# A hybrid attention layer on one core: maxima from a score pass of their own, exponentials with keys on the partitions

## The chip, the cores and the metric

The kernel runs on one core of one Trainium2 chip. The metric is the device time of one execution in microseconds (us), the median of several runs. TensorE (PE) multiplies matrices, VectorE (DVE), ScalarE (ACT) and GpSimd (POOL) do elementwise work, SyncE (SP) issues the DMAs.

## What is computed

One decoder layer over 2048 tokens of width 1024, in float32. A normalised input goes through one combined projection; three groups of heads read it: a causal pooling mixer, eight heads of forgetting attention, and four heads of cross-attention to 256 memory tokens. Each group is gated, the results are joined and go through an output projection, and the input is added.

```python
q = rms_norm(to_heads(q_b, FOX_HEADS), fox_q_g[l])        # 8 heads of 64
logits = einsum('bhqd,bhkd->bhqk', qi, k) * scale
logits = logits + Fi[..., None] - F[:, :, None, :]        # F = cumsum(log forget gate)
logits = where(causal, logits, -1e30)
p = softmax(logits, axis=-1)                              # one maximum and one sum per query
out = einsum('bhqk,bhkd->bhqd', p, v)
```

The memory heads do the same without F and mask. The scales of the norms are large, so the scores are too, and every softmax needs the maximum of its row.

## The kernel before, in words

Every float32 operand is split in two float16 halves (hi and lo), and a product is made of three matmuls (hi·hi, hi·lo, lo·hi), so that TensorE works in float16.

The work is cut into 16 units: four passes p over the columns of the projection (two attention heads, one memory head and one pooling group in each), and in each four blocks j of 512 queries. For a unit, `proj` makes q, k, v and gates of 512 tokens (line 714 has its matmuls, tiles pa and pb); `transpose_in` brings q and k into Q and K with the head's dimension on the partitions, by DMA transposes; then `attention` goes over three heads, h = 2 (memory), 0 and 1.

For one head `pieces` cuts the scores into pieces of up to 1024 columns, each in a buffer q of PSUM of which there are two ("qk": 2). `scores` fills it with queries on the partitions: for up to 512 keys one matmul of the high halves (line 1139, contraction 67: 64 dimensions and three rows with the forget sums F), one with the other halves (line 1144), and on the diagonal one that adds the mask (line 1142). `soften` finds the minimum of the negated scores per query on VectorE (line 1160; line 1156 for memory heads), makes a bias nm of it (lines 1164 and 1168), and takes the exponential on ScalarE with that bias (line 1175) into p, float32. `halves` writes p as ph: a cast by ScalarE or VectorE (lines 1195 and 1198) and a subtraction by VectorE or GpSimd (line 1202). Since the product with V needs keys on the partitions, ph goes through a DMA transpose into pt on SP's queue (line 1208). `weigh` multiplies pt and V, three matmuls of 64 or 65 columns per block of 128 queries by 128 keys (lines 1238 to 1240), into pv. Heads with more than 1024 keys do this in two parts with two biases, merged by `part` and `finish` (lines 1257 and 1272).

The order of all instructions is written by a planner, `Order`, before the program is built. It keeps a clock for each engine, with costs from a table, and two streams: `lead` (projections, then the output projection) and `follow` (attention), which may lag 1.1 units behind. A stream that has nothing ready lets the other go. Each engine then runs its instructions in that order, and an instruction that waits holds all behind it on its engine.

```python
COST = {"A": (0.08, 0.00086), "V": (0.07, 0.00105), "G": (0.1, 0.002), "C": (0.07, 0.00053), "S": (0.0, 1.0 / 360e3)}
...
            t = o.use("V", w // 2)
```

The table (line 39) gives microseconds, fixed and per column, of ScalarE (A), VectorE (V), GpSimd (G) and a cast on VectorE (C, by which an engine is chosen; line 1196, quoted second, is what that cast is then charged).

Of the kernel before, what the change touches and what calls it, by code (L numbers as in the profile page):

```python
# [10 lines left out]
F32 = mybir.dt.float32  # L11
# [25 lines left out]
ONE = 2.0 ** 14  # L37

# [162 lines left out]
class Layer:  # L201
    DEEP = 7
    BUFS = {
        "x": 3, "st": 4, "w": 2, "b": 2, "pj": 2, "qk": 2, "pv": 2, "p32": 3, "ph": 5, "pt": 6, "qkr": 2, "qsq": 2,
        "gate": 7, "z": 3, "kk": 1, "Q": 2, "cs": 2, "pw": 1, "hy": 3, "band": 1, "rx": 4, "cs2": 2, "early": 3, "late": 2, "scaled": 1,
# [19 lines left out]
    def setup(self):  # L225
# [33 lines left out]
        self.qq = kv.tile([P, 3, 4, P], F16, name="qq")  # L259
        self.fd = self.dr.tile([3 * NF, S], F16, name="fd")  # L260
# [497 lines left out]

    def mem_heads(self):
# [36 lines left out]
        def rest():  # L796
# [28 lines left out]
            nc.gpsimd.memset(self.Km[HD:HD + 3, 0], 0.0)  # L825
# [178 lines left out]
    def transpose_in(self, n, gates, normed):  # L1004
        nc, o = self.nc, self.o
        p, j = divmod(n, NJ)
        if p == 0:
            yield from self.wait(("forget", j))
        yield from o.until(lambda: 0 in normed and 1 in normed)
        if n > 0:  # L1010
            yield from self.wait("mem")
        else:
            yield from self.wait(("x", 1, 0))
            yield from self.wait(("x", 1, 1))
            yield from self.wait(("x", "mem", 0))
# [4 lines left out]
        Q, K = self.Q[n % 2], self.K[n % (NJ + 1)]  # L1020
        fs = self.fd[6 * p:6 * p + 6, j * TB:(j + 1) * TB].rearrange("(h c) s -> c h s", c=3)
# [6 lines left out]
        if n < 2:  # L1028
            nc.gpsimd.memset(Q[HD:HD + 3, 0], -1.0)
            nc.gpsimd.memset(Q[HD:HD + 1, 0], -1024.0)  # L1030
            o.use("G", 0, 1.5)
# [86 lines left out]
    def scores(self, n, h, piece, qk):  # L1118
# [7 lines left out]
        for i, k0, w, off in piece:  # L1126
            q1, q2 = Q1[:, h, i * P:(i + 1) * P], Q2[:, h, i * P:(i + 1) * P]
            for b in range(0, w, TB):
# [10 lines left out]
                nc.tensor.matmul(out, q1, kb, start=bank not in used, stop=False, **kw)  # L1139
                used.add(bank)  # L1140
                if diag:
                    nc.tensor.matmul(out[:, bw - P:], self.identb, self.mask, start=False, stop=False, **kw)
                    cost += 0.056
                nc.tensor.matmul(out, q2, ka, start=False, stop=True, **kw)  # L1144
                cost += 2 * bw / 2400.0 + 0.006
# [43 lines left out]
    def halves(self, n, h, c, w, p32, pt, place, head):  # L1189
# [14 lines left out]
        o.give(pt)  # L1204
        tt = yield from o.claim(place[2])
# [7 lines left out]
    def weigh(self, job):  # L1213
# [5 lines left out]
        g = piece[0][1] // HK  # L1219
# [7 lines left out]
        end = c == head["count"] - 1 or head["flat"][c + 1][0][1] // HK != g  # L1227
        T, nb, tt = head["box"].pop(c)
        b = 0
        for i, k0, w, off in piece:  # L1230
            for s in range(k0 // P, (k0 + w) // P):
                if h < 2:
                    v = self.V[(p * NJ + s // 4) % (NJ + 2)][:, s % 4, h, :]
                else:
                    v = self.Vm[:, s, p, :]
                ph, pl = T[:, b, :], T[:, nb + b, :]
                hi = v[:, HD:2 * HD + 1]
                nc.tensor.matmul(pv[:, i, :], ph, hi, start=start and b == 0, stop=False, **kw)  # L1238
                nc.tensor.matmul(pv[:, i, 0:HD], ph, v[:, 0:HD], start=False, stop=False, **kw)  # L1239
                nc.tensor.matmul(pv[:, i, :], pl, hi, start=False, stop=end and b == nb - 1, **kw)  # L1240
                b += 1
                if b % 2 == 0 or b == nb:
                    yield 0.0885 * (2 - b % 2)
# [53 lines left out]
    def attention(self):  # L1297
# [12 lines left out]
        def ready():  # L1310
            return late and late[0][2] in late[0][-1]["box"]

        for n in range(n_units):
            p, j = divmod(n, NJ)
            while n not in self.att_in or (n == 0 and "mem" not in self.done):
# [4 lines left out]
            gates, qt = self.att_in.pop(n)  # L1320
            first = True
            for h in (2, 0, 1):
                pieces = self.pieces(j, h)
                subs, count = [], 0
                for piece in pieces:
                    subs.append([])
                    for sub in self.cut(piece):
                        subs[-1].append((count, sub))
                        count += 1
                head = {  # L1330
                    "mn": self.sm.tile([P, 2, 4], F32, tag="mn", bufs=3, name=f"mn{n}{h}"),
                    "nm": self.sm.tile([P, 2, 4], F32, tag="nm", bufs=3, name=f"nm{n}{h}"),
                    "pv": {}, "box": {}, "subs": subs, "count": count, "gates": gates, "last": h == 1,
                    "flat": [sub for group in subs for _, sub in group],
                }
                for c, piece in enumerate(pieces):
                    while not o.free_slot("qk") or len(late) > self.DEEP:
                        if ready():
                            yield from drain()
                        else:  # L1340
                            yield -0.05
                    tk = o.first("qk")
                    qk = self.ps_qk.tile([P, 1024], F32, tag="qk", name=f"q{n}{h}{c}")
                    cost = self.scores(n, h, piece, qk)
                    o.spawn(self.soften((n, h, c, piece, qk, tk, head)), cost + SEM)
                    late += [(n, h, k, sub, head) for k, sub in subs[c]]
                    yield cost
                    if first:
                        first = False
                        o.spawn(self.pool_mix(p, j, gates))  # L1350
                    if ready():
                        yield from drain()
            o.give(qt)
            self.scored = n + 1
            o.spawn(self.store_mixed(n, gates))
# [6 lines left out]
    def follow(self):  # L1362

        n, spent = 0, 0.0
        for c in self.attention():
            spent += max(c, 0.0)
            total = 0.203 * (8 + 2 * (16 * (n % NJ) + 10))
# [238 lines left out]
```

## Time and profile before

| | |
|---|---|
| median of 3 runs | 1105.33 us (1098.9 to 1107.97) |
| the profiled execution | 1104.63 us |
| its span, first to last instruction | 1102.8 us |
| mean granted TensorE clock | 0.977 of 2.4 GHz |
| busy: PE, DVE, ACT, POOL | 1000.0, 817.5, 562.1, 433.0 us |

The times of the trace are from the profiled execution, one run. A busy time counts an engine's bars; bars of matmuls overlap, since they are pipelined. A wait is idle time of an engine just before an instruction, put down to what released it.

### The profile page before, as it was taken

The page shows a single profiled execution, that of the slowest core. Times are in us where ns is not written, and L with a number is a line of the kernel's source. Part 1 is how long each engine was busy: PE and PEld are TensorE (multiplying, and loading weights), DVE is VectorE, ACT ScalarE, POOL GpSimd, SP SyncE. Part 2 cuts the span into 40 slices and gives each one's busy share as a digit, 9 for nine tenths or more (in the row PEclk, how much of TensorE's full clock was granted, in tenths as well). Part 3 has the DMA queues.
Part 4 walks back from the last instruction along what each step waited for, and adds up shares of the span by engine and source line. Part 5 has one row for each costly group of instructions (what it writes and reads, how often), then busy time and mean ns, then how long its engine had stood idle before and what let it go on. Part 6 is the DMA issues. An engine that isn't in the chain of part 4 may idle for free.

```text
span 1102.8 us, 23610 instructions
## 1 busy us (share of the span) xinstructions
PE 1000.0 (91%) x8693; PEld 600.3 (54%) x8693; DVE 817.5 (74%) x1895; ACT 562.1 (51%) x1453; POOL 433.0 (39%) x484
## 2 busy tenths in 40 slices
PE   6798897889889998888899899998898989999998
PEld 3455564556556555555566565565555644444443
DVE  5977577599889797978887868998788796762111
ACT  4775466466646474656564656664555553430000
POOL 5543534354343643434345445543444460221000
PEclk8899698999999999999999999999999999999999
DMA  9889889999899998998998889999999699998521
GB/s 284 208 221 198 205 217 205 240 220 172 163 213 191 231 241 157 176 202 157 202 194 232 176 188 198 206 205 194 219 251 218 148 170 244 225 225 224 191 95 49
DMA packets 485700, 219.33 MB, mean 199 GB/s; under 512 B 442128, under 2 KB 450256, under 8 KB 484560
## 3 DMA queue, kind: packets, MB, share of 16 engines
q1 hardware_dynamic: 485440, 217.81, 91.4%
q8 instruction: 68, 1.11, 0.4%
q14 instruction: 48, 0.39, 0.1%
q10 hardware_dynamic: 144, 0.01, 0.0%
HBM read 84.23 MB, written 25.26 MB: 99 GB/s over the span
## 4 chain that ended last, share of the span: by engine, by line
PE 23%; DMA 12%; DVE 11%; issue 2%; SPq 1%; ACT 1%; POOL 1%; DVEq 0%; ACTq 0%; POOLq 0%
PE po L714 12%; DMA pt<-ph 12%; PE pa L714 4%; PE pb L714 3%; DVE mn L1160 3%; DVE ph L1202 2%; DVE ph L1195 1%; PE pv L1238 1%; PE q L1139 1%; PE q L1144 1%; PE pv L1240 1%; PE pv L1239 1%; SPq L1208 1%; POOL ph L1202 1%; DVE qq L998 1%
## 5 line engine op out<-in xcount | busy, mean ns | idle before, releaser
L1175 ACT ACTIVATE p<-q,nm 128x512 f32<-128x512 f32 (+3 forms) x384 | 216.3, 601 | 168.0 <-DVE nm L1168 79.6
L714 PEld LDWEIGHTS <-x 128*128 128x128 f16 x2304 | 216.1, 98 | 130.1 <-issue 4.7
L714 PE MATMUL pa<-ah,x 128*128 128x512 f16 x768 | 250.1, 382 | 0.0
L1202 POOL TENSOR_TENSOR ph<-p,ph 128x512 f16<-128x512 f32 (+3 forms) x115 | 134.6, 1175 | 259.2 <-DVE ph L1195 148.3
L1238 PE MATMUL pv<-v,pt 128*128 128x65 f16 x1088 | 130.8, 194 | 56.5 <-DMA pt<-ph 56.1
L1160 DVE TENSOR_REDUCE mn<-q 128x1 f32<-128x128 f32 (+2 forms) x192 | 170.7, 902 | 6.8 <-PE q L1144 6.6
L1202 DVE TENSOR_TENSOR ph<-p,ph 128x512 f16<-128x512 f32 (+3 forms) x221 | 159.5, 732 | 18.1 <-ACT ph L1198 16.5
L1238 PEld LDWEIGHTS <-pt 128*128 128x128 f16 x1216 | 114.3, 99 | 105.0 <-DMA pt<-ph 89.9
L714 PE MATMUL po<-aho,om 128*128 128x512 f16 x512 | 157.9, 379 | 0.0
L714 PE MATMUL pa<-al,x 128*128 128x512 f16 x384 | 146.5, 381 | 0.0
L714 PE MATMUL pb<-bh,x 128*128 128x256 f16 x768 | 140.8, 273 | 1.6 <-DVE v L925 1.5
L1198 ACT CAST ph<-p 128x512 f16<-128x512 f32 (+3 forms) x168 | 97.2, 586 | 72.5 <-DMA pt<-ph 58.2
L1239 PE MATMUL pv<-v,pt 128*128 128x64 f16 x1088 | 130.3, 194 | 0.0
L1240 PE MATMUL pv<-v,pt 128*128 128x65 f16 x1088 | 129.9, 195 | 0.0
L1139 PE MATMUL q<-k,q 67*128 67x512 f16 (+2 forms) x320 | 111.1, 350 | 13.6 <-ACT p L1175 8.8
L1239 PEld LDWEIGHTS <-pt 128*128 128x128 f16 x1216 | 113.9, 98 | 16.8 <-issue 0.8
L714 PEld LDWEIGHTS <-om 128*128 128x128 f16 x768 | 73.3, 98 | 83.7
L1240 PEld LDWEIGHTS <-pt 128*128 128x128 f16 x1216 | 114.2, 98 | 0.0
L1144 PE MATMUL q<-k,q 128*128 128x512 f16 (+2 forms) x320 | 110.8, 349 | 0.0
L970 POOL TENSOR_TENSOR rr<-ss,mhalf 128x10 f32<-128x10 f32 x32 | 65.4, 2044 | 103.1 <-DVE ss L965 99.0
L714 PE MATMUL pb<-bl,x 128*128 128x256 f16 x384 | 105.0, 273 | 0.0
L1195 DVE CAST ph<-p 128x512 f16<-128x512 f32 (+3 forms) x168 | 77.2, 468 | 35.3 <-DMA pt<-ph 30.8
(244 smaller groups left out, 1750.0 us busy)
## 6 DMA issues: line engine op xcount, KB each, us to landing
x<-xd SPq DMA_DIRECT2D x48, 512.0 KB
xrx<-in_x SPq DMA_DIRECT2D x16, 512.0 KB
xd<-xx SPq DMA_DIRECT2D x16, 512.0 KB
md<-mt SPq DMA_DIRECT2D x32, 256.0 KB
om<-md SPq DMA_DIRECT2D x8, 1024.0 KB
xo<-in_x SPq DMA_DIRECT2D x16, 512.0 KB
out_dram<-xo SPq DMA_DIRECT2D x32, 256.0 KB
w0a<-in_w_a SPq DMA_DIRECT2D x12, 512.0 KB
```

The lines of the kernel that those rows point to most:

```text
L714: nc.tensor.matmul(out, rows, r[kt][:, :ncol], start=(kt == 0 and i == 0), stop=(kt == KT - 1 and i == 2))
L970: nc.gpsimd.tensor_tensor(rr, ss, self.mhalf[:, 0:10].rearrange("p (a b) -> p a b", b=5), op=ALU.pow)
L1139: nc.tensor.matmul(out, q1, kb, start=bank not in used, stop=False, **kw)
L1144: nc.tensor.matmul(out, q2, ka, start=False, stop=True, **kw)
L1160: nc.vector.tensor_reduce(mn[:, g, i:i + 1], qk[:, off:off + w], axis=AX.X, op=ALU.min)
L1175: nc.scalar.activation(p32[:, at:at + w], qk[:, off:off + w], AF.Exp, bias=nm[:, g, i:i + 1], scale=-1.0)
L1195: nc.vector.tensor_copy(hl[:, :w], p32[:, :w])
L1198: nc.scalar.copy(hl[:, :w], p32[:, :w])
L1202: (nc.vector if eng == "V" else nc.gpsimd).tensor_tensor(hl[:, w:2 * w], p32[:, :w], hl[:, :w], op=ALU.subtract)
L1238: nc.tensor.matmul(pv[:, i, :], ph, hi, start=start and b == 0, stop=False, **kw)
L1239: nc.tensor.matmul(pv[:, i, 0:HD], ph, v[:, 0:HD], start=False, stop=False, **kw)
L1240: nc.tensor.matmul(pv[:, i, :], pl, hi, start=False, stop=end and b == nb - 1, **kw)
```

## The change

Every head now has two score passes. The first (`scores` with `peak`) has the high halves and the mask alone, with queries on the partitions, and gives only the minima (`peak`). Two float16 rows are made of them (in a tile mz, 128 columns wide per block of queries), turned by four matmuls with an identity (tile mp), and copied into rows 96 and 97 of Q by ScalarE or VectorE; K has the matching constants there (`extra_rows`, memsets on GpSimd). The second pass (`turned_scores`) has keys on the partitions, all halves, and a contraction of 98 rows, so the maximum comes out subtracted; `spread` takes the exponentials with one constant bias, in full banks of 512 where it can. The halves ph are then read by `weigh` as weights; no pt is made of them and no DMA transpose is issued for them. A head has one part whatever its keys. The first pass of the next head goes ahead of the second pass of this one (AHEAD = 1). There are nine buffers ph in place of five.

```diff
-        "x": 3, "st": 4, "w": 2, "b": 2, "pj": 2, "qk": 2, "pv": 2, "p32": 3, "ph": 5, "pt": 6, "qkr": 2, "qsq": 2,
+        "x": 3, "st": 4, "w": 2, "b": 2, "pj": 2, "qk": 2, "pv": 2, "p32": 3, "ph": 9, "pt": 6, "qkr": 2, "qsq": 2,
...
+    def extra_rows(self, K):
+        nc, o = self.nc, self.o
+        nc.gpsimd.memset(K[HD:P, 0], 0.0)
+        nc.gpsimd.memset(K[MAX_ROW:MAX_ROW + 2, 0], 1.0)
+        nc.gpsimd.memset(K[MAX_ROW:MAX_ROW + 1, 0], 1024.0)
+        o.use("G", 0, 3.0)
...
+    def columns(self, j, h):
+        if h == 2:
+            return [[[(0, 0, TB)], [(1, 0, TB)]]]
+        k = 4 * j
+        full = [[[(b, 0, TB)], [(b + 1, 0, TB)]] for b in range(0, k, 2)]
+        return full + [[[(k, 0, TB)], [(k + 1, P, 3 * P), (k + 3, 3 * P, P)]], [[(k + 2, 2 * P, 2 * P)]]]
+
+    def turned_scores(self, n, h, piece, qk):
...
+                nc.tensor.matmul(out, k1, Q1[:, q0:q0 + w], start=i == 0, stop=False, **kw)
+                if h < 2 and kb >= 4 * j:
+                    nc.tensor.matmul(out[:, 0:P], self.mask, self.identb, start=False, stop=False, **kw)
+                nc.tensor.matmul(out, k2, Q2[:, q0:q0 + w], start=False, stop=True, **kw)
...
+    def peak(self, n, h, c, piece, qk, tk, head):
...
+                nc.vector.tensor_reduce(mn[:, g, i:i + 1], qk[:, off:off + w], axis=AX.X, op=ALU.min)
...
+        if g:
+            nc.vector.tensor_tensor(n0, n0, mn[:, 1, :], op=ALU.min)
+        nc.vector.tensor_scalar(mz[:, :, MAX_ROW], n0, -1.0 / 1024.0, None, op0=ALU.mult)
+        nc.vector.scalar_tensor_tensor(
+            mz[:, :, MAX_ROW + 1], mz[:, :, MAX_ROW], -1024.0, n0, op0=ALU.mult, op1=ALU.subtract
+        )
...
+        for t in range(4):
+            nc.tensor.matmul(mp[:, t * P:(t + 1) * P], mz[:, t], self.identh, start=True, stop=True)
...
+        (nc.scalar.copy if eng == "A" else nc.vector.tensor_copy)(self.Q[n % 2][rows, 0, h], mp[rows])
...
+    def spread(self, n, h, c, piece, qk, tk, head):
...
+            nc.scalar.activation(p32[:, :w], qk[:, b * TB:b * TB + w], AF.Exp, bias=self.lnp, scale=-1.0)
...
     def halves(self, n, h, c, w, p32, pt, place, head):
...
+        if head["turned"]:
+            head["box"][c] = (hl.rearrange("p (b c) -> p b c", c=P), w // P, ht)
+            return
...
+            for ahead in todo[:self.AHEAD + 1]:
+                if ahead["n"] not in self.att_in or (ahead["n"] == 0 and "mem" not in self.done):
+                    break
+                if ahead["todo"]:
+                    step = ahead
+                    break
+            if step is None and n in self.att_in and ("mem" in self.done or n) and (not head["turned"] or "peaked" in head):
+                step = head
```

The order extracts below show how instructions stand in the built program; a number behind a name is that of one buffer.

TensorE before, in unit 10 (p = 2, j = 2): a piece of scores (tile q, L1139 and L1144) of head 0, then the projection (pa).

```order
L1139 LDWEIGHTS q_124
L1139 MATMUL q_9699<-k_116,q_124 128x512
L1144 LDWEIGHTS q_124
L1144 MATMUL q_9699<-k_116,q_124 128x512
L1139 LDWEIGHTS q_124
L1139 MATMUL q_9699<-k_117,q_124 128x512
L1144 LDWEIGHTS q_124
L1144 MATMUL q_9699<-k_117,q_124 128x512
L714 LDWEIGHTS x_7_8794
```

TensorE after, at the same head's second pass (q_124 holds its queries): the last of the four matmuls that turn the maxima of the next head (mp), a piece with keys as weights (L1166, L1170), and the first product with V, with ph as weights.

```order
L1204 LDWEIGHTS mz_130
L1204 MATMUL mp_9878<-identh,mz_130 128x128
L1166 LDWEIGHTS k_117
L1166 MATMUL q_4_9890<-q_124,k_117 128x512
L1170 LDWEIGHTS k_117
L1170 MATMUL q_4_9890<-q_124,k_117 128x512
L1166 LDWEIGHTS k_117
L1166 MATMUL q_4_9890<-q_124,k_117 128x512
L1170 LDWEIGHTS k_117
L1170 MATMUL q_4_9890<-q_124,k_117 128x512
L1353 LDWEIGHTS ph_9883
L1353 MATMUL pv_9900<-v_120,ph_9883 128x65
```

Scores before have the queries as weights and the keys streaming; after, the keys are the weights and the queries stream. The products with V read ph where they read pt, and the turning of the next head's maxima stands in the middle of this head's pieces.

VectorE before, in unit 8: the minima of a piece (mn), the bias that ScalarE waits for (nm), and the weight splits of the next pass (bl).

```order
L1160 TENSOR_REDUCE mn_8099<-q_8187 128x1 x3
L1168 TENSOR_SCALAR nm_8100<-mn_8099 128x3
L1202 TENSOR_TENSOR ph_8220<-p_8172,ph_8220 128x512
L467 SCALAR_TENSOR_TENSOR bl_8017<-w1b_7932,wgkb_7929,bh_8016 128x192
L467 SCALAR_TENSOR_TENSOR bl_8017<-w1b_8018,wgkb_7929,bh_8016 128x192
L1160 TENSOR_REDUCE mn_8099<-q_8242 128x1
L1168 TENSOR_SCALAR nm_8100<-mn_8099 128x1
```

VectorE after, in the same unit: the last minima of a head, then two splits, then the pair that makes the rows for the turning (mz).

```order
L436 TENSOR_SCALAR Sz_p<-cs2z_8336 128x1
L1184 TENSOR_REDUCE mn_8291<-q_2_8325 128x1
L474 SCALAR_TENSOR_TENSOR bl_8123<-w1b_8084,wgkb_8081,bh_8122 128x192
L641 SCALAR_TENSOR_TENSOR bl_8123<-wz_8265,wgz_8283,bh_8122 128x8x64
L1196 TENSOR_SCALAR mz_130<-mn_8291 128x4
L1197 SCALAR_TENSOR_TENSOR mz_130<-mz_130,mn_8291 128x4
L474 SCALAR_TENSOR_TENSOR bl_8123<-w1b_8084,wgkb_8081,bh_8122 128x192
```

Before, the bias stands right behind its reduction. After, two weight splits stand between the last reduction and the pair, and TensorE's four matmuls wait for the pair.

## Rows read from the trace of the kernel before

**Rows 1.** The page, part 1: busy us, share of the span, instructions of each engine.
```profile
PE 1000.0 (91%) x8693; PEld 600.3 (54%) x8693; DVE 817.5 (74%) x1895; ACT 562.1 (51%) x1453; POOL 433.0 (39%) x484
```

**Rows 2.** Stretches: window, length, busy us of PE, PEld, DVE, ACT, POOL; clock, DMA share.
```profile
0.00:165.40 165.40, 140.97 (x834) 82.14 (x835) 118.14 (x300) 97.18 (x242) 80.72 (x99) 0.91 0.88 222
165.40:992.50 827.10, 752.61 (x7312) 469.05 (x7311) 680.95 (x1569) 463.12 (x1209) 349.22 (x381) 0.99 0.99 202
992.50:1102.80 110.30, 106.37 (x550) 49.15 (x548) 18.41 (x27) 1.75 (x3) 3.10 (x4) 1.00 0.44 140
220.50:358.40 137.90, 125.90 (x1331) 83.00 (x1329) 127.26 (x300) 83.65 (x221) 58.37 (x61) 1.00 0.98 192
```

**Rows 3.** What TensorE waited for: us in total, times, longest us.
```profile
PE pv L1238 <- DMA pt<-ph: 59.6, 62, 3.2
PE q L1139 <- ACT p L1175: 8.8, 12, 2.1
```

**Rows 4.** Timeline of TensorE at 502 us: start us, bar us, instruction.
```profile
502.46 0.38 PE L1139 MATMUL q<-k,q 67*128 67x512 f16 x1
502.68 0.38 PE L1144 MATMUL q<-k,q 128*128 128x512 f16 x1
502.90 0.27 PE L1139 MATMUL q<-k,q 67*128 67x256 f16 x1
503.01 0.22 PE L1142 MATMUL q<-mask,identb 128*128 128x128 bf16 x1
503.07 0.27 PE L1144 MATMUL q<-k,q 128*128 128x256 f16 x1
503.18 0.19 PE L1238 MATMUL pv<-v,pt 128*128 128x65 f16 x1
503.21 0.19 PE L1239 MATMUL pv<-v,pt 128*128 128x64 f16 x1
```

**Rows 5.** The same timeline at the three longest DMA waits; in brackets the wait.
```profile
121.19 0.24 PE L1238 MATMUL pv<-v,pt 128*128 128x65 f16 x1 [3.19 <-DMA pt<-ph]
...
179.34 0.24 PE L1238 MATMUL pv<-v,pt 128*128 128x65 f16 x1 [3.11 <-DMA pt<-ph]
...
417.74 0.24 PE L1238 MATMUL pv<-v,pt 128*128 128x65 f16 x1 [3.19 <-DMA pt<-ph]
```

**Rows 6.** Slices of 27.57 us (columns as in Rows 2) whose granted clock falls.
```profile
110.28:137.80 27.52, 22.75 (x149) 14.97 (x148) 15.49 (x49) 13.01 (x34) 14.48 (x20) 0.69 0.90 206
...
165.42:193.00 27.58, 21.15 (x193) 12.79 (x192) 20.32 (x59) 17.37 (x42) 13.12 (x16) 0.88 0.99 205
...
413.55:441.10 27.55, 24.36 (x204) 14.89 (x203) 19.37 (x46) 12.82 (x38) 8.85 (x9) 0.94 0.83 157
...
523.83:551.40 27.57, 24.10 (x231) 15.34 (x228) 22.26 (x59) 14.69 (x37) 9.61 (x10) 0.94 1.09 202
```

**Rows 7.** First score matmuls by shape: count, busy us, mean ns, idle before.
```profile
L1139 PE MATMUL q<-k,q 67*128 67x512 f16 x224 | 85.5, 382 | 11.0 <-ACT p L1175 7.9 <-DVE nm L1168 2.1 <-DVE nm L1164 0.9
...
L1139 PE MATMUL q<-k,q 67*128 67x384 f16 x32 | 10.6, 332 | 0.0
...
L1139 PE MATMUL q<-km,q 67*128 67x256 f16 x64 | 15.1, 273 | 0.5 <-DVE q L1033 0.5
...
L1142 PE MATMUL q<-mask,identb 128*128 128x128 bf16 x128 | 28.2, 221 | 0.0
```

**Rows 8.** VectorE work on scores by shape, in the same columns.
```profile
L1202 DVE TENSOR_TENSOR ph<-p,ph 128x512 f16<-128x512 f32 x173 | 134.4, 788 | 14.7 <-ACT ph L1198 13.7
...
L1195 DVE CAST ph<-p 128x512 f16<-128x512 f32 x118 | 60.3, 520 | 26.1 <-DMA pt<-ph 22.6 <-ACT p L1175 3.1 <-DMA mt<-mh 0.2
...
L1160 DVE TENSOR_REDUCE mn<-q 128x1 f32<-128x1024 f32 x80 | 97.2, 1215 | 3.8 <-PE q L1144 3.6
...
L1168 DVE TENSOR_SCALAR nm<-mn 128x1 f32<-128x1 f32 x104 | 16.0, 154 | 3.6
```

**Rows 9.** The page, part 5: all first score matmuls together; after the bar the idle time.
```profile
L1139 PE MATMUL q<-k,q 67*128 67x512 f16 (+2 forms) x320 | 111.1, 350 | 13.6 <-ACT p L1175 8.8
```

More of the change, by code (lines that the diff above doesn't have):

```diff
@@ L1027, in transpose_in @@
         tk = o.use("S", 0, 0.9)
[L1028 to L1031, printed above, removed]
         yield from o.at(tq)
@@ new lines, in spread @@
+    def spread(self, n, h, c, piece, qk, tk, head):
+        nc, o = self.nc, self.o
+        subs = head["subs"][c]
+        places = [[o.reserve(tag) for tag in ("p32", "ph")] for _ in subs]
+        for b, ((k, sub), place) in enumerate(zip(subs, places)):
+            w = sum(x[2] for x in sub)
+            pt = yield from o.claim(place[0])
+            p32 = self.pp.tile([P, TB], F32, tag="p32", bufs=self.BUFS["p32"], name=f"p{n}{h}{k}")
+            nc.scalar.activation(p32[:, :w], qk[:, b * TB:b * TB + w], AF.Exp, bias=self.lnp, scale=-1.0)
+            t = o.use("A", 1.0 * w + 180)
+            o.spawn(self.halves(n, h, k, w, p32, pt, place, head), t - o.now)
+        yield from o.at(t)
+        o.give(tk)
@@ L1120, in scores @@
+    def scores(self, n, h, piece, qk, peak=False):
         nc = self.nc
@@ L1204, in halves @@
         o.give(pt)
+        if head["turned"]:
+            head["box"][c] = (hl.rearrange("p (b c) -> p b c", c=P), w // P, ht)
+            return
         tt = yield from o.claim(place[2])
@@ L1218, in weigh @@
         kw = dict(skip_group_check=True)
-        g = piece[0][1] // HK
+        part = lambda sub: 0 if head["turned"] else sub[0][1] // HK
+        g = part(piece)
         if g not in head["pv"]:
@@ L1226, in weigh @@
         pv = head["pv"][g][0]
-        end = c == head["count"] - 1 or head["flat"][c + 1][0][1] // HK != g
+        end = c == head["count"] - 1 or part(head["flat"][c + 1]) != g
         T, nb, tt = head["box"].pop(c)
[L1229 to L1243, printed above, removed]
+        if head["turned"]:
+            blocks = [(i, k) for k, q0, w in piece for i in range(q0 // P, (q0 + w) // P)]
+        else:
+            blocks = [(i, k) for i, k0, w, off in piece for k in range(k0 // P, (k0 + w) // P)]
+        for b, (i, k) in enumerate(blocks):
+            v = self.V[(p * NJ + k // 4) % (NJ + 2)][:, k % 4, h, :] if h < 2 else self.Vm[:, k, p, :]
+            ph, pl, hi = T[:, b, :], T[:, nb + b, :], v[:, HD:2 * HD + 1]
+            nc.tensor.matmul(pv[:, i, :], ph, hi, start=start and b == 0, stop=False, **kw)
+            nc.tensor.matmul(pv[:, i, 0:HD], ph, v[:, 0:HD], start=False, stop=False, **kw)
+            nc.tensor.matmul(pv[:, i, :], pl, hi, start=False, stop=end and b == nb - 1, **kw)
+            if b % 2 or b == nb - 1:
+                yield 0.0885 * (1 + b % 2)
         o.give(tt)
@@ L1319, in attention @@
                     yield -0.05
[L1320 to L1343, printed above, removed]
-                    cost = self.scores(n, h, piece, qk)
[L1345 to L1352, printed above, removed]
@@ L1356, in attention @@
+            if ready():
+                yield from drain()
         while late:
@@ L1366, in follow @@
             spent += max(c, 0.0)
-            total = 0.203 * (8 + 2 * (16 * (n % NJ) + 10))
+            total = 0.2 * (8 + 2 * (16 * (n % NJ) + 10))
+            total += sum(0.06 * (8 if h == 2 else 16 * (n % NJ) + 10) + 0.23 for h in range(3) if self.turned(n % NJ, h))
             if spent > total and n < NSW * NJ - 1:
```

142 lines of the change are left out of this document (129 added, 13 removed).

## The prediction

> **What bounds the kernel now.** I read the busy shares first, then the stretches of the span, then what TensorE waited for, then its timeline. TensorE is busy 91% of the span and VectorE 74% [rows 1]. The span falls into three stretches: 165 us of start, 827 us in which projections and attention are interleaved, and 110 us of output projection [rows 2]. The change lies almost wholly in the middle one. There TensorE is busy 752.6 of 827.1 us, so 74.5 us are idle; VectorE is busy 82%, and the DMA engines' share is 0.99. So the DMA engines look full. But what a full queue costs is read from who waits for it: TensorE waited 59.6 us, 62 times, for a transposed piece of the exponentials [rows 3], and little for anything else.
>
> Is a busy TensorE busy in earnest? The timeline of an attention piece says yes: the starts of its matmuls are 0.22 us apart after 512 columns, 0.11 after 256 and 0.06 after the mask's 128, with no gap [rows 4]. The bars are longer (0.38 us) and overlap, so I price by distances of starts, not by bars.
>
> The Trainium skill ("Trainium Kernel Development and Optimization", section Performance Expectations) says that matmul busy time is a bad measure of distance from the roofline, and that the share of weight loads is a good one. Weight loads are busy 54% here [rows 1]; by that rule 46% of TensorE would be free and the added pass would hide. The starts of rows 4 speak against it: a 512-column matmul holds the array while its next weights are loaded. It stays as a rival below.
>
> **The change part by part.**
>
> *Added on TensorE.* Every head gets a first pass with the high halves alone, for the maxima. It has as many matmuls as one of the two passes of before: 224 of 512 columns, 32 each of 384, 256 and 128, 64 of 256 for the memory heads, and 128 masks again [rows 7]. At the distances of rows 4 (384 columns taken as 0.16): 224 x 0.217 + 32 x 0.16 + 96 x 0.11 + 32 x 0.06 + 128 x 0.06 = 48.6 + 5.1 + 10.6 + 1.9 + 7.7 = 74 us. Then four matmuls of 128 columns per head turn the maxima into rows: 48 x 4 x 0.06 = 11.5. Together 85 us. The second pass with keys on the partitions has the same columns as the score pass of before (448 of 512 columns again; 64 of 512 for the memory heads, where 128 of 256 were), and the products with V read their weights from ph in place of pt, 3648 as before: no difference. Nothing hides the 85 us: TensorE is the engine they are put on, and its idle time in the middle stretch is shorter than that.
>
> *Removed: 336 DMA transposes.* The queue keeps only the plain transfers and the transposes of q, k, x and the gated rows. With them go the 59.6 us of waits [rows 3]. Those waits also cost clock: the granted clock falls to a mean of 0.69, 0.88, 0.94 and 0.94 in four slices [rows 6], part of each slice being at 1.2 in place of 2.4 GHz, and three of the four hold a wait of over 3 us [rows 5]. Lost: 27.5 x (0.31 + 0.12 + 0.06 + 0.06) = 15 us; I give all of it back, with 0 and 18 as ends (18 if two more slices at 0.94 are counted, which hold shorter waits).
>
> *A new wait, on the score buffers.* There are still two, and each is now filled twice as often: 176 fills for maxima beside 176 for exponentials. TensorE waited 13.6 us for 176 fills on these buffers [rows 9]; I add as much again, 14 us. Ends: 0 (the maxima give their buffer back after one reduction, without exponentials) and 28.
>
> *A new chain per head.* The last reduction (1.22 us for 1024 columns, rows 8), two small operations on VectorE, four matmuls, and a copy of two rows to Q must be over before the head's second pass. In before the exponentials alone waited for the maxima, on ScalarE; now TensorE does, and with it every projection matmul queued behind. In the order of VectorE after, the pair stands behind two weight splits of the next pass. The cover is the next head's first pass and the projections, so I price the chain itself at 0. Uncovered it would be some 3 us (an estimate: the reduction, two operations of 0.15 to 0.2 like the nm row of rows 8, the matmuls and the copy) for each of 48 heads, 144 us, which is an end that I think far off: the next head's first pass alone is 3.1 us in the longest units (58 blocks of 0.054) and 0.5 us in the shortest.
>
> *Late halves in place of late transposes.* The piece is now read by TensorE as soon as VectorE or GpSimd has written it. The program's order was made with 0.34 + 0.61 us for cast and subtraction on VectorE (its cost table); the trace has 0.52 + 0.79 [rows 8]. That is 0.36 us later than planned; in 62 places (the waits of before) this is 22 us at most. I take half, 11 us; ends 0 and 60 (all waits of before stay, with another releaser).
>
> *VectorE and the rest.* By the counts of the order, casts on VectorE rise from 168 to 215 and subtractions from 221 to 242, all but 32 of them full width: at 0.52 and 0.79 about +30 and +27 us. The nm operations (16 us for the 104 narrow ones of rows 8, some 30 in all) and the merging of two partial outputs (about 17) go; the 48 pairs of small operations, 16 joins of two maxima and 16 of the copies to Q come, about +26 us. Net +36 us on VectorE, 681 to some 717 in the middle stretch. If that stretch grows to 860 us this is 83%, as now, so I charge nothing. GpSimd loses 37 of its 115 subtractions and gets some memsets; ScalarE's casts fall from 168 to 105 while its exponentials become 320 wider ones in place of 384. Neither bounds.
>
> *Sum.* The profiled execution took 1104.6 us, within 0.1% of the median of the three runs (1105.3). 1104.6 + 85 - 60 - 15 + 14 + 11 = 1140 us, slower by 3%. (About 1% is what a measurement of this kernel can tell from no change.)
>
> **The rivals.**
>
> 1. *A draw.* The removal also frees the engines that feed TensorE: the exponentials no longer wait for VectorE, and the casts no longer for buffers that the DMA held. Then neither new wait comes: 1104.6 + 85 - 75 = 1115, at the edge of no difference. For it: few of TensorE's waits now have another cause than the transposes. Against: VectorE gets more work, not less.
>
> 2. *Faster: the DMA queue was the bound of the middle stretch.* Its share is 0.99 there [rows 2]. If everything that TensorE waits for there hangs on it, all 74.5 us go, the 15 of the clock too, and the 62 drains of 0.17 us that count as busy (a 65-column matmul shows 0.19 to 0.20 us but is followed after 0.03, rows 4): 1104.6 + 85 - 74.5 - 15 - 10.5 = 1090. It wins from the point at which TensorE shows under 10 us of waits between the first head and the last. By the weight-load share as measure of room, TensorE takes the 85 us into its idle time: 1104.6 - 75 = 1030. That is the skill's rule of above; I give it 2 in 100 of this case.
>
> 3. *Slower still: VectorE becomes the bound.* From 220 to 358 us it is already busy 127.3 of 137.9 us, 92% [rows 2], in heads with many keys beside the weight splits. If it is the limit in such places, its added 36 us come on top of TensorE's, less the 6 or so that fall elsewhere: 1140 + 30 = 1170. It decides from the point at which VectorE is over 90% busy over the whole middle stretch. Against: the two largest waits of TensorE in that stretch [rows 3] are on others.
>
> 4. *The change doesn't do what it says.* The order shows 336 transposes gone from SP and every head with a first pass; no chance.
>
> **How the numbers follow.** Forecast 0.50, with a range of its own from 1117 to 1160; the draw 0.20; the faster case 0.15; VectorE 0.15. The time is that of the forecast, 1140. The range for 8 in 10 takes in most of the draw and reaches to the two other cases: 1093 to 1172, whose upper end also holds all 60 us of late halves less the clock's return. Faster by over 1% has the 0.15 of the second rival; within 1% the 0.20 of the first and a little of the forecast's lower edge, 0.22; slower 0.63.
>
> **What would show it right or wrong.** Right: about 85 us more of matmul starts; no wait of TensorE for a DMA in the middle stretch; the granted clock at 1.00 after the first 60 us; waits of the score matmuls for VectorE and ScalarE of some 25 to 30 us, and of the V products for ph of some 10; the DMA share of the middle stretch at half or less. The forecast fails if the middle stretch gets no longer than 830 us (the draw or the faster case), if TensorE waits for the copied rows at the start of many heads (the chain is not covered), or if VectorE's busy share there passes 90% (third rival). The step that I trust least is the price of the new waits, 25 us between 0 and 88.

## The result, and the profile after

The changed kernel took 1118.38 us (median of 4 runs, 1115.19 to 1120.38), the kernel before 1105.42 on the same chip: a ratio of 1.013, 95% interval 1.009 to 1.017. The direction was right (slower), the size was not: 3.1% was forecast, 1.3% came. The profiled execution took 1120.38 us, with a span of 1118.5 us and a mean clock of 0.991.

The page, part 1, of the changed kernel, as [rows 1]:

```profile
PE 1066.6 (95%) x9333; PEld 647.6 (58%) x9333; DVE 841.6 (75%) x1884; ACT 540.7 (48%) x1342; POOL 403.3 (36%) x452
```

TensorE is busy 66.6 us more and idle 50.9 us less (51.9 of the span against 102.8); the difference is the 15.7 us by which the span grew.

The same stretches as [rows 2], and below them the two later slices (of 28 us) in which the clock is not at 1.00:

```profile
0.00:165.40 165.40, 143.50 (x936) 84.86 (x937) 127.65 (x318) 101.41 (x251) 89.56 (x110) 0.96 0.82 216
165.40:992.50 827.10, 801.03 (x7833) 507.54 (x7833) 695.88 (x1543) 439.33 (x1092) 313.73 (x342) 1.00 0.38 106
992.50:1118.50 126.00, 122.07 (x566) 55.16 (x564) 18.02 (x24) 0.00 (x0) 0.00 (x0) 1.00 0.39 131
...
531.24:559.20 27.96, 27.29 (x170) 16.19 (x169) 18.26 (x60) 9.34 (x35) 11.57 (x13) 0.94 0.79 223
699.00:727.00 28.00, 26.59 (x190) 15.20 (x188) 26.19 (x47) 9.35 (x29) 8.93 (x11) 0.94 0.64 174
```

In the middle stretch TensorE is now busy 97%, VectorE 84%; the DMA share fell from 0.99 to 0.38.

Attention is not over later than before: its last product with V starts at 984.9 us, where it was 1006.7. The added work shows at the end. The planner fills gaps of TensorE with the output projection (tile po); of its 768 matmuls some 286 fell in the middle stretch before, and 204 do now. What is left runs alone, in the chain of waits of the changed kernel (start us, us):

```profile
985.07 129.51 PE po L721 x600
```

Each of the two later slices with a lowered clock holds a wait of TensorE for mz, the pair of small operations on VectorE (start us, bar us, in brackets the wait):

```profile
552.71 1.97 PE L614 MATMUL zp<-pw,ut 64*128 64x64 f32 x16 [0.67 <-DVE mz L1197]
...
718.15 0.40 PE L1204 MATMUL mp<-identh,mz 128*128 128x128 f16 x4 [1.28 <-DVE mz L1197]
```

Around the second one the granted clock is 0.82 from 717 to 720 us and 0.61 from 720 to 723.

What TensorE waited for, as [rows 3] (us in total, times, longest us):

```profile
PE pv L1355 <- DVE ph L1315: 9.7, 20, 1.4
PE warm_pj L1667 <- ACT k L379: 8.3, 1, 8.3
PE q L1166 <- ACT p L1223: 5.5, 8, 1.4
...
PE mp L1204 <- DVE mz L1197: 3.3, 5, 1.3
...
PE q L1166 <- DVE mn L1184: 2.1, 3, 0.9
PE q L1250 <- DVE mn L1184: 1.8, 3, 1.3
PE pv L1355 <- POOL ph L1315: 1.7, 4, 0.6
```

No wait for a transposed piece is left. The V products (pv) wait 11.4 us for ph, from VectorE and GpSimd; the score buffers (q) cost 10.6 us with two short lines not shown; the turning of the maxima (mp) 3.5 us.

The timeline of TensorE in a first pass, as [rows 4] (start us, bar us, instruction):

```profile
430.75 0.22 PE L1250 MATMUL q<-k,q 67*128 67x128 f16 x1
430.81 0.22 PE L1253 MATMUL q<-mask,identb 128*128 128x128 bf16 x1
430.87 0.27 PE L1250 MATMUL q<-k,q 67*128 67x256 f16 x1
430.98 0.22 PE L1253 MATMUL q<-mask,identb 128*128 128x128 bf16 x1
431.04 0.33 PE L1250 MATMUL q<-k,q 67*128 67x384 f16 x1
431.20 0.22 PE L1253 MATMUL q<-mask,identb 128*128 128x128 bf16 x1
431.27 0.38 PE L1250 MATMUL q<-k,q 67*128 67x512 f16 x1
431.49 0.22 PE L1253 MATMUL q<-mask,identb 128*128 128x128 bf16 x1
```

After 128, 256, 384 and 512 columns the next start is 0.06, 0.11, 0.16 and 0.22 us away, as priced. From start to next start, without waits, all 704 added matmuls of the trace (first pass and turning) take 85.6 us.

VectorE's work on scores by shape, as [rows 8]:

```profile
L1315 DVE TENSOR_TENSOR ph<-p,ph 128x512 f16<-128x512 f32 x225 | 164.8, 755 | 2.1 <-ACT ph L1311 0.3
...
L1308 DVE CAST ph<-p 128x512 f16<-128x512 f32 x200 | 95.6, 494 | 8.1 <-ACT p L1223 7.7
...
L1184 DVE TENSOR_REDUCE mn<-q 128x1 f32<-128x1024 f32 x80 | 96.1, 1216 | 4.2 <-PE q L1250 2.5 <-PE q L1253 1.4
```

The added casts and subtractions came as counted, each a little shorter than before (494 and 755 ns, 520 and 788 before). VectorE's busy time grew by 24.1 us in all, where 36 were priced.

The account of the two profiled executions, from these views:

| term | forecast us | measured us |
|---|---|---|
| first pass and turning | +85 | +85.6 by starts |
| waits for pt | −60 | −59.6 |
| clock, (1 − granted) x span: 25.4, then 10.1 | −15 | −15.3 |
| waits for score buffers: 11.8, then 10.6 | **+14** | **−1** |
| V products waiting for ph | +11 | +11.4 |
| chain per head (mp) | 0 | +3.5 |
| all other waits of TensorE: 26.5, then 20.7 | 0 | −6 |
| sum | +35 | +18.6 (the span: +15.7) |

### The profile page after: what moved, and what is told of

Its sections match the earlier page's. It is cut to its first block, busy times and chain, and to the rows that moved or that the text cites. A ratio compares the mean times of both kernels' runs of the same rounds, so it can differ in the third digit from the quotient of the medians.

```text
span 1118.5 us, 23634 instructions
## 1 busy us (share of the span) xinstructions
PE 1066.6 (95%) x9333; PEld 647.6 (58%) x9333; DVE 841.6 (75%) x1884; ACT 540.7 (48%) x1342; POOL 403.3 (36%) x452
## 4 chain that ended last, share of the span: by engine, by line
PE 61%; DVE 26%; ACT 4%; DMA 4%; issue 3%; POOL 1%; SPq 1%; ACTq 0%; DVEq 0%; POOLq 0%
PE pa L721 18%; PE po L721 14%; PE pb L721 10%; DVE ph L1315 5%; DVE mn L1184 4%; PE q L1250 4%; DVE ph L1308 4%; PE q L1166 3%; PE q L1170 3%; PE pv L1355 2%; PE pv L1353 2%; PE pv L1354 2%; DVE al L474 1%; ACT p L1223 1%; DMA w0b<-in_w_b 1%
## 5 line engine op out<-in xcount | busy, mean ns | idle before, releaser
L1223 ACT ACTIVATE p<-q,lnp 128x512 f32<-128x512 f32 (+1 forms) x320 | 202.2, 667 | 126.6 <-PE q L1170 71.6
L1315 POOL TENSOR_TENSOR ph<-p,ph 128x512 f16<-128x512 f32 (+1 forms) x78 | 95.9, 1233 | 264.0 <-DVE ph L1308 131.7
L1315 DVE TENSOR_TENSOR ph<-p,ph 128x512 f16<-128x512 f32 (+1 forms) x242 | 172.3, 737 | 2.2 <-ACT ph L1311 0.3
L1355 PE MATMUL pv<-v,ph 128*128 128x65 f16 x1088 | 120.2, 194 | 11.8 <-DVE ph L1315 8.9
L1355 PEld LDWEIGHTS <-ph 128*128 128x128 f16 x1216 | 111.3, 97 | 18.6 <-DVE ph L1315 14.9
L1353 PEld LDWEIGHTS <-ph 128*128 128x128 f16 x1216 | 113.8, 98 | 13.8 <-issue 0.3
L1353 PE MATMUL pv<-v,ph 128*128 128x65 f16 x1088 | 121.4, 193 | 0.0
L1354 PE MATMUL pv<-v,ph 128*128 128x64 f16 x1088 | 121.3, 192 | 0.0
L1354 PEld LDWEIGHTS <-ph 128*128 128x128 f16 x1216 | 112.3, 97 | 13.2 <-issue 0.2
L1166 PE MATMUL q<-q,k 98*128 98x512 f16 (+1 forms) x320 | 111.3, 348 | 7.6 <-ACT p L1223 5.5
L1170 PE MATMUL q<-q,k 128*128 128x512 f16 (+1 forms) x320 | 109.4, 346 | 0.0
L1619 DVE SCALAR_TENSOR_TENSOR xo<-po,So_p,xo 128x512 f32<-128x512 f32 x32 | 24.0, 749 | 110.4 <-PE po L721 110.4
L1308 DVE CAST ph<-p 128x512 f16<-128x512 f32 (+1 forms) x215 | 100.4, 484 | 8.1 <-ACT p L1223 7.7
```

What stands on the lines that cost most here:

```text
L1166: nc.tensor.matmul(out, k1, Q1[:, q0:q0 + w], start=i == 0, stop=False, **kw)
L1170: nc.tensor.matmul(out, k2, Q2[:, q0:q0 + w], start=False, stop=True, **kw)
L1223: nc.scalar.activation(p32[:, :w], qk[:, b * TB:b * TB + w], AF.Exp, bias=self.lnp, scale=-1.0)
L1308: nc.vector.tensor_copy(hl[:, :w], p32[:, :w])
L1315: (nc.vector if eng == "V" else nc.gpsimd).tensor_tensor(hl[:, w:2 * w], p32[:, :w], hl[:, :w], op=ALU.subtract)
```

## The experiments

Two theories stood at the start. A: the added pass costs its 85 us on a full TensorE, and what the transposes give back (waits and clock) is less; the rest are small new waits. B, the rival: the added pass is nearly free, and what costs is something else in the new code. Ratios are to the kernel before, measured on the same chip; its medians were 1107.3 to 1107.9 us, and 1104.7 for the last four. How the same work is planned moves the time too: with no head turned the new loop and its nine buffers cost 0.7%, and a copy that was only added (both below) took 0.5% off. So a difference of that size is put down to no single part.

**None turned, half turned.** `turned` decides whether a head uses the new way (`True`) or the way of before, in the new code.

```diff
     def turned(self, j, h):
-        return True
+        return False        # none_turned
+        return h == 1       # half_turned
```

> The changed kernel with no head turned: one score pass, DMA transposes again, but with the new planner loop, nine buffers ph and the added constants. Theory (the first pass and the transposes are the whole change): 1105 us within 1%, TensorE waits for transposed pieces some 60 us again, DMA share of the middle stretch about 1. Rival (part of the gain came from nine buffers ph): 1090 us or less, with under 35 us of waits for transposed pieces.

> Only head 1 of each unit is turned: 544 of 1216 blocks. Added on TensorE: 544 x 0.054 + 64 x 0.06 + 16 x 0.24 = 37 us. Theory (the waits of before come from a full DMA queue): with 55% of the transposes the share of the middle stretch falls to about 0.7, the waits for transposed pieces from 60 to about 10 us, the clock gives back about 12: 1105 + 37 - 50 - 12 = 1080 us. Rival (the waits go with the number of transposed pieces): 55% stay, 1105 + 37 - 27 - 7 = 1108 us.

None turned: 1115.98 us, 1.007 (1.003 to 1.011), at the upper edge of what was expected; in the profiled execution, its longest (1126.31 us), TensorE waits 62.4 us for pt again, at a DMA share of 0.98 in the middle stretch. Half turned (a third of the heads, with 45% of the blocks of scores): 1097.89 us, 0.991 (0.988 to 0.995), faster than either whole. The waits of TensorE with half the heads turned:

```profile
PE pv L1353 <- DMA pt<-ph: 28.7, 32, 2.2
PE warm_pj L1667 <- ACT k L379: 7.7, 1, 7.7
PE q L1250 <- DVE mn L1184: 5.8, 7, 1.5
```

The DMA share of the middle stretch is 0.72 here, so the queue is not full, and yet 28.7 us of waits for pt are left. The theory had expected 10. This is what its rival expected: each of the 184 transposes that are left costs TensorE as much wait as each of the 336 before, 0.16 us against 0.18. Within the new code, turning every head rather than none costs 0.6% (the two intervals overlap); the rest of the 1.3% is there with no head turned and belongs to the new plan as a whole.

**The first pass issued twice.**

```diff
-                cost = self.scores(n, h, piece, qk, True)
+                cost = self.scores(n, h, piece, qk, True) + self.scores(n, h, piece, qk, True)
```

> The changed kernel with every matmul of the first pass issued twice into the same columns: 74 us more on TensorE and nothing else. Theory (TensorE is the bound, a matmul costs what it streams): 1118 + 74 = 1192 us, between 1180 and 1200. Rival (there is room on TensorE, the first pass hides in idle time; also what the weight-load share of 58% would say): 1118 to 1150 us.

1247.69 us, 1.126 (1.119 to 1.133), more than the 1200 us expected at most. In the profiles the span grew from 1118.5 to 1241.5, by 123 us: idle time of TensorE +23, clock +31 ((1 − 0.967) x 1241.5 against 10.1), and 69 left for the doubled matmuls, priced at 74. So theory A holds for its largest term, and B falls. The page of this kernel, part 1:

```profile
PE 1166.2 (94%) x9845; PEld 702.5 (57%) x9845; DVE 856.5 (69%) x1902; ACT 544.3 (44%) x1344; POOL 375.7 (30%) x432
```

TensorE's weight loads are busy 57% of this span, 58% without the doubling: that share showed no room which the pass could use, against the rival that the prediction drew from the Trainium skill ("Trainium Kernel Development and Optimization", section Performance Expectations). The clock took more than expected; in slices of 3 us, columns as in [rows 2], of the kernel with the doubled pass:

```profile
847.00:850.00 3.00, 1.95 (x18) 1.08 (x16) 3.00 (x4) 0.58 (x1) 2.90 (x2) 0.81 0.08 30
850.00:853.00 3.00, 2.48 (x23) 1.39 (x21) 2.97 (x5) 1.40 (x5) 1.61 (x3) 0.50 0.00 0
853.00:856.00 3.00, 2.67 (x12) 1.35 (x11) 3.00 (x8) 0.00 (x0) 0.87 (x2) 0.50 0.00 0
856.00:859.00 3.00, 3.00 (x12) 1.42 (x11) 1.84 (x3) 0.00 (x0) 0.00 (x0) 0.50 0.00 0
859.00:862.00 3.00, 3.00 (x10) 1.16 (x9) 2.10 (x4) 0.00 (x0) 0.00 (x0) 0.50 0.00 0
```

VectorE is busy 2.97 to 3.00 us in the first three, TensorE waits for its reductions in pieces of 1.05 us and less, and the granted clock falls to 0.50 (1.2 GHz). Over the whole span this wait comes to 11.3 us (1.8 without the doubling):

```profile
PE q L1250 <- DVE mn L1184: 11.3, 15, 2.1
```


**The planner's costs set to what the trace shows.** The late halves were put down to a table that has casts and subtractions too short. In `halves`:

```diff
-            t = o.use("V", w // 2)
+            t = o.use("V", 0, real["C"])
...
-        yield from o.at(o.use(eng, w))
+        yield from o.at(o.use(eng, 0, real[eng]))
```

`real` is 0.23 + 0.00052w us for a cast on VectorE, 0.195 + 0.00083w on ScalarE, 0.225 + 0.00104w and 0.54 + 0.0015w for a subtraction on VectorE and GpSimd; the engine is chosen by it too.

> The changed kernel with the planner's costs of cast and subtraction set to what the trace shows (512 columns: cast 0.50 on VectorE, 0.62 on ScalarE; subtraction 0.76 on VectorE, 1.31 on GpSimd). Theory (products with V wait for ph because the plan has the halves too early): those waits fall from 11.4 us to under 4, 1110 us. Rival (they come from the queue on VectorE, whatever the plan says): waits of 8 to 15 us, 1118 us within 5.

1107.36 us, 1.000 (0.997 to 1.003), 11 us less than the changed kernel's median; its waits:

```profile
PE pv L1357 <- DVE ph L1317: 4.6, 9, 1.6
PE mp L1204 <- DVE mz L1197: 3.3, 7, 0.8
PE q L1250 <- DVE mn L1180: 2.4, 1, 2.4
PE q L1250 <- DVE mn L1184: 2.3, 7, 0.6
PE q L1166 <- ACT p L1223: 2.3, 6, 0.8
```

The waits for ph (with GpSimd's 1.9) are 6.5 us, 11.4 without the edit: between the theory's 4 and the rival's 8. That the late halves come from the plan's costs is thus borne out in direction; of the 13.4 us by which the span fell (to 1105.1), 8 are idle time and 5 busy time, and only 4.9 stand under ph.

The same costs in the kernel before, and in the one with half the heads turned:

> The kernel before with the planner's costs of cast and subtraction set to what the trace shows, as in e4. Theory (late halves are part of the 60 us of waits for transposed pieces): those fall below 50 us, about 1097 us. Rival (the transpose itself is what comes late, 3 to 8 us after its issue): 55 to 65 us stay, 1107 us within 4.

> Only head 1 turned, as in e2, with the planner's costs of e4. Theory (the two gains add): 0.991 - 0.010 of the kernel before, about 1085 to 1089 us. Rival (e2's remaining waits are for transposed pieces, which e4's costs do not touch): 1094 to 1098 us.

1100.78 us, 0.995 (0.991 to 0.998), and 1098.98 us, 0.991 (0.989 to 0.994). With the transposes there the true costs gain 0.5% or nothing, and the waits for pt do not fall: 66.9 us in the one (in its longest execution), 32.2 in the other.

**No chain.** In the changed kernel the pair of small operations, the four matmuls and the copy are left out, and the maxima are not subtracted.

```diff
-        zt = yield from o.take("mz")
...
-        o.give(zt)
...
-            nc.scalar.activation(p32[:, :w], qk[:, b * TB:b * TB + w], AF.Exp, bias=self.lnp, scale=-1.0)
+            nc.scalar.activation(p32[:, :w], qk[:, b * TB:b * TB + w], AF.Exp, bias=self.lnp, scale=-1e-4)
```

> The changed kernel without the chain from the maxima to Q: no rows are made, turned or copied, a second pass needs only its first pass to be over, and the exponentials are taken of scores scaled by 0.0001 with the maxima left in (that part of the computation is left out). 192 matmuls of 128 columns (11.5 us) and the small operations go. Theory (the chain is covered by the next head's first pass and by projections): 1118 - 11.5 - 4 of waits = 1102 us. Rival (the chain holds TensorE up through the order it forces, 0.5 us or more a head): under 1085 us.

1092.19 us, 0.985 (0.980 to 0.991), between the 1102 us of the theory and the 1085 of the rival. Its page, part 1:

```profile
PE 1047.2 (96%) x9141; PEld 635.1 (58%) x9141; DVE 817.1 (75%) x1777; ACT 514.5 (47%) x1297; POOL 402.8 (37%) x444
```

The span is 26.7 us shorter: 7 of idle time, 5 of clock (0.995), and 15 of busy time, 11.5 of which were priced for the turning matmuls. So 15 us went beyond these, where 0 was forecast: the 7 and the 5, and 3 of busy time. Only 3.5 us stand in the wait of the turning matmuls: most of it does not stand under the chain's own name. Some 3.4 us of it are not the chain's: the clock of the first 28 us, before any head, is 0.94 here and 0.82 in the changed kernel.

**Two heads ahead**, with the true costs, to give the chain more cover:

```diff
-    AHEAD = 1
+    AHEAD = 2
```

> The kernel of e4 (every head turned, true costs) with the first passes two heads ahead in place of one. Theory (the chain from the maxima to Q is not covered; f1 without it was 15 us faster than its matmuls account for): a part of the 15 us comes back, 1097 to 1102 us. Rival (those 15 us are the chain's work on VectorE and ScalarE, not its waits): 1107 us within 3.

1111.98 us, 1.002 (0.999 to 1.005), not faster than 1107.36 and above what either side expected; the wait for mz is 3.7 us, 3.3 with one head ahead. More cover of this kind gives nothing back.

**The score buffers.** Why do twice as many fills wait no longer? One theory: in before a buffer is held until the exponentials are done, which wait for the minima; the changed kernel gives the first pass's buffer back after one reduction. To free the buffer sooner in before, its exponentials got a constant bias (so the maxima are not subtracted) and the plan no longer holds them for the minima.

```diff
-        yield from o.at(o.use("V", 0, 0.17))
+        tv = o.use("V", 0, 0.17)
...
-                nc.scalar.activation(p32[:, at:at + w], qk[:, off:off + w], AF.Exp, bias=nm[:, g, i:i + 1], scale=-1.0)
+                nc.scalar.activation(p32[:, at:at + w], qk[:, off:off + w], AF.Exp, bias=self.lnp, scale=-1e-4)
...
-        yield from o.at(t)
+        yield from o.at(max(t, tv))
```

> The kernel before, with exponentials that do not wait for the minima: a constant bias and scores scaled by 0.0001 (the maxima are left in; the minima and biases are still computed). A score buffer is then held for the longer of reduction and exponentials, not for their sum; the number of fills stays 176. Theory (what TensorE waits for on score buffers goes with the time that a fill is held): its waits on them fall from 13.6 us to under 7, 1095 to 1107 us in all. Rival (they go with the number of fills, as the prediction had it): they stay at 12 to 15 us.

1121.3 us, 1.011 (1.004 to 1.018), and the buffers cost TensorE more, 22.3 us. What ScalarE waited for in this kernel:

```profile
ACT p L1177 <- DVE mn L1162: 182.0, 108, 6.7
ACT p L1177 <- DVE mn L1158: 53.9, 14, 7.0
```

ScalarE still waited for the reductions, though no value of theirs was used: as the program was built, the two reads of one buffer follow each other. So the edit did not free the buffer, and its planner reckoned with a freedom that was not there. The theory is not tested by it. It points to another one: the planner puts other work of TensorE where by its clock no buffer is free, so a wait shows where the plan has a buffer back too early. Here it had, and the waits doubled; with the true costs in the kernel before they fell from 11.8 to 5.1 us. No run tests this by itself.

The other theory: what counts is how many engines a buffer passes through. In the changed kernel an 8-column copy by ScalarE was put between the reduction and the return of the buffer.

```diff
         yield from o.at(o.use("V", 0, 0.05))
+        nc.scalar.copy(self.scr, qk[:, 0:8])
+        yield from o.at(o.use("A", 0, 0.2))
         o.give(tk)
```

> The changed kernel, in which a score buffer of the first pass is given back only after its reduction on VectorE and then a copy of 8 columns on ScalarE: 176 fills pass two engines, as every fill of the kernel before did, and 176 (second pass) one. Theory (waits on score buffers go with the passages through engine queues: 352 in the kernel before, 13.6 us; 352 in the changed one, 10.6 us): 528 passages, 16 to 20 us of waits, 1118 + 7 = 1125 us or more. Rival (they go with fills, or hang on something else): 8 to 13 us of waits, 1118 us within 4.

1114.47 us, 1.008 (1.004 to 1.011), and 6.0 us of waits for buffers: more passages, no more waits. That theory falls.

**Why transposes are waited for when the queue is not full.** With half the heads turned the share was 0.72, and for each transpose TensorE waited as before. The chain of waits of the kernel before shows how long those take that were waited for (start us, us):

```profile
533.23 4.07 DMA pt<-ph
537.38 5.38 DMA pt<-ph
...
565.11 6.49 DMA pt<-ph
...
927.14 8.43 DMA pt<-ph
```

With half the heads turned the pieces in the chain of waits are 3.3 to 5.8 us. There the trace also has the time from issue to landing for all 184:

```profile
DMA to landing us min/median/max: 2.3/3.5/6.2
```

The plan has 0.875 us of the queue for a full piece (w = 512, so 1024 columns with both halves); with its fixed parts for issue and landing that is some 3.0 us on an empty queue. That is under the median, so it puts many V products too early. An edit of its delay alone:

```diff
-MARGIN = 0
+MARGIN = 2.0
...
         yield from o.at(o.use("S", 0, 1.75 * w / 1024) + MARGIN)
```

It was run with several choices of heads (`turned`), with and without the true costs. The table has all of that family.

| kernel | heads turned | true costs | delay us | ratio (95%) | waits for pt us | DMA share, middle |
|---|---|---|---|---|---|---|
| before_margin (g2) | code of before | no | 2 | 0.997 (0.993 to 1.001) | 34.5 | 1.01 |
| none_margin (h1) | none | yes | 2 | 0.994 (0.990 to 0.998) | 36.8 | 1.02 |
| late_half_margin (h2) | h = 1 where j is 2 or 3 | yes | 2 | 0.985 (0.978 to 0.991) | 21.4 | 0.82 |
| half_margin (g4) | h = 1 | yes | 2 | **0.967 (0.963 to 0.972)** | 6.6 | 0.76 |
| half_margin_old (h4) | h = 1 | no | 2 | 0.987 (0.981 to 0.992) | 8.4 | 0.74 |
| more_margin (h3) | h = 1, and h = 0 where j is 3 | yes | 2 | 0.984 (0.979 to 0.989) | 0.2 | 0.63 |
| half, true costs (f4) | h = 1 | yes | 0 | 0.991 (0.989 to 0.994) | 32.2 | 0.73 |

> The kernel before with 2 us more in the planner for a DMA transpose's landing (its constant MARGIN), so that the products with V stand later in the order. Theory (TensorE waits because the plan has the transposes too early, as e2's 28.7 us at a DMA share of 0.72 suggest): waits for transposed pieces from 60 to under 35 us, about 1090 us. Rival (the full queue is the limit): they stay above 50 us, 1103 us or more.

> Only head 1 turned, true costs, and 2 us more for a transpose's landing. Theory (as g2): the waits for transposed pieces fall from 32 us (f4) to under 18, about 1085 us. Rival (full queue or buffers): 28 us or more, 1095 to 1100 us.

> No head turned, nine buffers ph, true costs, 2 us more for a transpose's landing: g4's plan with a full queue. Theory (both are needed): DMA share of the middle stretch 0.98 or more, 1095 to 1108 us. Rival (the plan with nine buffers is enough): 1085 us or less.

> As g4, but head 1 is turned only in units with j of 2 or 3: 400 of 1216 blocks, 25 us added on TensorE in place of 37, 67% of the transposes in place of 55%. Theory (g4's queue has room to spare): DMA share about 0.82, waits for transposed pieces under 12 us, 1065 to 1073 us. Rival (the room is used up): waits of 20 us or more, 1080 us or more.

> As g4, with head 0 turned too in units with j = 3: 776 of 1216 blocks, 15 us more on TensorE, 36% of the transposes. Theory (g4 has removed what waits there are to remove, so more turning only costs its matmuls): 1076 + 15 - 4 = 1087 us. Rival (the transposes still cost more than they show): 1076 us or less.

> As g4 with the planner's old costs of cast and subtraction. Theory (what matters is the landing and the room in the queue; the costs bring what they brought in e4 at half the heads, 5 us): 1078 to 1084 us. Rival (the plan must have all its costs right to gain): 1090 us or more.

The delay alone, on a full queue, takes the waits from 59.6 [rows 3] to 34.5 us and the time by nothing that can be told. What was saved comes back elsewhere: TensorE is idle 100.0 us in all, 102.8 without the delay, and the clock is 0.969 against 0.977. In before with the delay:

```profile
PE pv L1238 <- DMA pt<-ph: 34.5, 37, 3.1
PE pa L714 <- DMA xx<-k: 10.2, 3, 4.6
```

Room in the queue alone leaves 28.7 to 32.2 us, hardly less for each transpose than on the full queue. Both together leave 6.6: 0.04 us for each transpose, where the delay alone leaves 0.10 and the room alone 0.16 to 0.18. And with the true costs this is the fastest kernel of the study, 1075.8 us (1075.25 to 1079.04), 3.3% under the kernel before. Its page, part 1, then its middle stretch, and its waits:

```profile
PE 1014.8 (95%) x8981; PEld 617.8 (58%) x8981; DVE 824.4 (77%) x1838; ACT 556.0 (52%) x1426; POOL 470.0 (44%) x502
```

```profile
165.40:992.50 827.10, 799.83 (x7766) 503.26 (x7764) 693.31 (x1525) 457.63 (x1180) 379.28 (x392) 0.99 0.76 168
```

```profile
PE warm_pj L1669 <- ACT k L379: 7.9, 1, 7.9
PE pv L1355 <- DMA pt<-ph: 6.6, 12, 1.4
```

TensorE is as busy in the middle as in the changed kernel (799.8 against 801.0 us), but it has less to do: 288 matmuls more than before [rows 1], where the changed kernel has 640 more. The next three mixes are slower than it by 1.7 to 2%. With fewer heads turned the queue fills again (h2). With more, TensorE pays for first passes that no wait repays: the waits for pt fall only from 6.6 to 0.2 us (h3). Without the true costs 2% are lost (h4), more than expected. Of the 15 us by which that span is longer, 1.8 stand in the waits for pt and some 2 in those for ph; how much of the rest is the costs and how much the luck of one plan is not shown.

## Why the prediction was wrong in size

- **The 85 us on TensorE: right.** The starts are as far apart as priced, 85.6 us in all, and doubling the pass cost 69 us of streaming beside waits and clock. The prediction's sign for them, a middle stretch of over 830 us, did not come: attention ended 22 us sooner, and output projection was pushed to the end in its place.
- **The waits for pt and their clock: right**, −59.6 and −15.3 against −60 and −15. The clock is not quite at 1.00 after the start: two slices stand at 0.94, each with a wait for the new chain (mz) in it.
- **The score buffers: this is the step that failed.** "I add as much again, 14 us" priced a wait per fill, from 13.6 us that were all idle time before these matmuls (11.8 of them for a buffer). Twice the fills cost 10.6 us where half as many had cost 11.8: −1 in place of +14. In all kernels but two of the study the buffers cost 5 to 13 us, whatever the number of fills (the two: the doubled pass, 25, and the constant bias in before, 22.3). What sets these waits stays open: the trial on how long a buffer is held did not free it, the number of passages is not it, and that the plan has buffers back too early is a guess from two runs.
- **Late halves: right**, 11.4 us against 11, and smaller with mended costs. That it came so close is luck: half of an upper bound was taken.
- **The chain per head at 0: too low.** Its wait is 3.5 us, and some 3.4 us of clock stand in the two slices with its waits. No wait for the copied rows themselves shows. Leaving the chain out gives back 15 us beyond its matmuls, of which 3.4 are clock at the start and a mere new plan could make up to 8 (the 0.7% of above); the rest was not separated.
- **The other waits at 0:** they fell by 6 us. With the buffers' 15, less the 3.5 of the chain, this is 17 of the 19 us between the forecast's +35 and the span's +15.7; the terms as measured still add up to 3 us more than the span grew.
- **VectorE not the bound: right.** It is busy 84% in the middle, 90% was the point for the third rival. Its added work was less than priced (24.1 us of 36). That TensorE's clock falls at waits for it was not foreseen; it shows at mz, and more with the doubled pass.
- **The draw** (1115 us) came nearest in time. Its reason is half right: of the two new waits the one on the score buffers did not come, the one for ph did.
- **The faster rival**, that the full queue bounds the middle stretch: the queue was emptied to 0.38 and the kernel got slower. The waits for pt were the plan's as well as the queue's, which shows only when both are mended.

## What to carry to other kernels

A transfer that shows up as a wait can be late because its queue is full or because the plan calls for it too soon; mending one alone may give nothing, so test both together before removing the transfer. Where a full TensorE pays for relieving another resource, relieve only as much as is waited for: a third of the heads was enough here, with the plan mended. Do not price a wait on a pair of buffers from how often they are filled: twice the fills cost no more here.

## What was not expected of the hardware

The granted clock fell to 0.50 (1.2 GHz) while TensorE was far from idle: with the doubled first pass it was busy 1.95 and 2.48 of 3 us as the clock fell, between waits of 1.05 us and less, and the clock stayed at 0.50 through two slices in which TensorE was busy 3.00 of 3.00 us. In the changed kernel it fell behind a single wait of 1.28 us (0.61 from 720 to 723 us). In the kernel before, three of the four slices of [rows 6] held a single wait of over 3 us [rows 5]. And a DMA transpose in the chain of waits takes 3.2 to 8.4 us with the queue full and still 3.3 to 5.8 us at a share of 0.72: the longest get shorter with room, the shortest do not.
